# Linear attention on one core: weights cleared in eight parts, and in the tail half of a second matmul ahead of two pieces of TensorE work

## The chip, the core and the metric

The kernel runs on one core of a Trainium2 chip. A core has five engines that run side by side, each with its own instruction queue: PE (TensorE, matrix products), DVE (VectorE), ACT (ScalarE), POOL (GpSimd) and SP (SyncE, used here for issuing transfers only). Sixteen DMA engines move data between HBM and the on-chip memory (SBUF); PE writes its results to PSUM. The metric is the device time of one execution in microseconds (us), lower is better. Before the change the median of five runs is 127.72 us.

## What is computed

Linear attention over 8 x 12 = 96 heads of 512 positions and 64 features, all in fp32 at the interface:

```python
Q_feat = np.maximum(0, Q) + 1
K_feat = np.maximum(0, K) + 1
KV = np.einsum('bhkd,bhkv->bhdv', K_feat, V)
K_sum = np.sum(K_feat, axis=2)
numerator = np.einsum('bhqd,bhdv->bhqv', Q_feat, KV)
denominator = np.einsum('bhqd,bhd->bhq', Q_feat, K_sum)
return numerator / (denominator[:, :, :, None] + 1e-10)
```

Per head there is a first product (K features with V, a 64 x 64 matrix, and the sum of the K features beside it) and a second one (Q features with that matrix), and then each row is divided by its denominator.

## The kernel before

**Tiles and groups.** The 96 heads are taken in 12 groups (NG, 0 to 11) of 8 heads. Two groups make a pair, which is loaded together. Groups 2 to 9 are "eights": their Q rows are laid out so that two groups share one transposed tile, and the two groups' outputs interleave in HBM. Groups 0, 1, 10 and 11 stand by themselves.

**Steps of a group.** `k_features` and `q_features` apply max(x, 0) + 1 on DVE (written as max(x + 1, 1)). `v_blocks` spreads V into a block layout, three blocks by DVE and one by ACT. `keys_values` is the first matmul: 32 products of 64 x 320 on PE into PSUM, which ACT then casts into `kva_all`, the weights of the second matmul, four slots (`kva_diag`) used in turn. Only the diagonal blocks of a slot are written, so the rest of `kva_all` is cleared once at the start, by a memset on POOL (L274). `transposes` turns the Q features on PE, in two halves of eight transposes; ACT copies each half from PSUM to `qt`, but for the second half of group 11, which DVE copies (L213). `output` is the second matmul and the division. In each of two halves h it issues 16 matmuls of 128 x 130 into two PSUM tiles, and DVE then takes for each tile a reciprocal (L241) and a multiply (L242) into the output tile `o_sb`. There are two such PSUM tiles in all, so a half's matmuls wait for the multiplies of the half before.

**Transfers.** Loads and the stores of groups 0 to 9 are issued by POOL (L109, L119, L141); a load converts fp32 to bf16 on the way. The first K load and the stores of groups 10 and 11, each in two pieces of 512 KB, are issued by SP (L101, L144). Input tiles have two buffers per pair, output tiles six (OUT_BUFS), one for each group.

**Order.** The order on each engine is that of the program. Group g of the loop transposes what is due, makes features and V blocks of g, does the output of g - 2, the first matmul of g, issues the loads of the pair after the next, and stores g - 3. The last passes are written out:

```python
            if g == last - 1:
                v_blocks(g)
                k_features(last)
                v_blocks(last)
...
        q_features(last - 1)
        transposes(last - 1)
        q_features(last)
        output(last - 2)
        keys_values(last)
        transposes(last)
        output(last - 1)
        output(last)
```

Here `last` is 11. So PE's tail is: first matmul of 10, transposes of 10, second matmul of 9, first matmul of 11, transposes of 11, second matmul of 10, second matmul of 11.

Of the kernel before, what the change touches and what calls it, by code (L numbers as in the profile page):

```python
# [8 lines left out]
FP32 = mybir.dt.float32  # L9
BF16 = mybir.dt.bfloat16  # L10
ALU = mybir.AluOpType

BANK = 512
IN_BUFS = 2
OUT_BUFS = 6
LAG = 3


# [1 line left out]
def kernel(  # L20
# [21 lines left out]
    nc = tc.nc  # L42

    B, H, S, D = Q.shape
    P = 128
    C = 8
# [3 lines left out]
    NP = 4  # L50
    NG = NPAIR // NP
    D1 = D + 1
    W = 2 * D1
# [15 lines left out]
    mid_pool = ctx.enter_context(tc.tile_pool(name="mid", bufs=2))  # L69
    out_pool = ctx.enter_context(tc.tile_pool(name="out_pool", bufs=OUT_BUFS))  # L70
    recip_pool = ctx.enter_context(tc.tile_pool(name="recip", bufs=4))
    psum_kva = ctx.enter_context(tc.tile_pool(name="psum_kva", bufs=2, space=bass.MemoryType.PSUM))
    psum = ctx.enter_context(tc.tile_pool(name="psum", bufs=2, space=bass.MemoryType.PSUM))
# [3 lines left out]
    NV = 4  # L77
# [4 lines left out]
    kva_all = const.tile([P, NV, 4, 2, D1], BF16, name="kva_all")  # L82
    kva_diag = [kva_all[:, i] for i in range(NV)]
# [5 lines left out]
    qfs = {}  # L89
    qts = {}  # L90
    outs = {}

    def eights(g):
        return 2 <= g < NG - 2
# [4 lines left out]
    def load_first_k():  # L99
        k_raw = head_pool.tile([P, 2, C2, D], FP32, name="k_first")  # L100
        nc.sync.dma_start(out=k_raw, in_=k_dram[:, 0:2])  # L101
        raw["k", 0] = k_raw
# [29 lines left out]
                load("q", (g,))  # L132

    def store(g):
        o_sb = outs.pop(g)
        first = 2 * NP * (g // 2)
        o_to = o_dram[:, first + g % 2 : first + 2 * NP : 2] if eights(g) else o_dram[
            :, g * NP : g * NP + NP
        ]
        if g < NG - 2:  # L140
            nc.gpsimd.dma_start(out=o_to, in_=o_sb)  # L141
            return
        for h in range(2):
            nc.sync.dma_start(out=o_to[:, h:NP:2], in_=o_sb[:, h:NP:2])  # L144
# [13 lines left out]
    def v_blocks(g):  # L158
        v_raw = raw.pop(("v", g))
        for b in range(4):  # L160
            ps = slice(32 * b, 32 * b + 32)
            if b == 3:
                nc.scalar.copy(out=v_blk[g % 2][ps, b], in_=v_raw[ps])  # L163
            else:
                nc.vector.tensor_copy(out=v_blk[g % 2][ps, b], in_=v_raw[ps])  # L165
# [11 lines left out]
    def keys_values(g):  # L177
        kf = kfs.pop(g)
        sb = g % 2
        vb = v_all[:, 4 * sb : 4 * sb + 5]  # L180
        kva_ps = psum_kva.tile([P, 5, D], FP32, name="kva_ps")
        for c in range(C2):
            for n in range(2):
                nc.tensor.matmul(  # L184
                    kva_ps[64 * n : 64 * n + 64],
                    lhsT=kf[:, c, n, :],
                    rhs=vb[:, :, n, c, :],
                    start=(c == 0),
                    stop=(c == C2 - 1),
                )  # L190
        kva = kva_diag[g % NV]
        for n in range(2):
            ps = slice(64 * n, 64 * n + 64)
            nc.scalar.copy(out=kva[ps, :, n, 0:D], in_=kva_ps[ps, sb : sb + 4, :])  # L194
            nc.scalar.copy(out=kva[ps, :, n, D], in_=kva_ps[ps, 4 - 4 * sb, 0:4])  # L195

    def transposes(g):
        qf = qfs.pop(g)
        R, CC = qf.shape[1:3]
        if R == 4 and g % 2:  # L200
            qts[g] = qts[g - 1]
        else:
            qts[g] = mid_pool.tile([P, C, P, R], BF16, name=f"qt{R}")
        first = g % 2 * CC if R == 4 else 0
        for half in range(2):
            qt_ps = psum_qt.tile([P, CC // 2, R, P], BF16, name="qt_ps")
            for c in range(CC // 2):
                for r in range(R):
                    nc.tensor.transpose(  # L209
                        qt_ps[:, c, r], qf[:, r, half * CC // 2 + c, :, :], identity  # L210
                    )
            lo = first + half * CC // 2
            copy = nc.vector.tensor_copy if half and g == NG - 1 else nc.scalar.copy  # L213
            copy(out=qts[g][:, lo : lo + CC // 2], in_=qt_ps.rearrange("p c r q -> p c q r"))  # L214

    def output(g):
        qt = qts.pop(g)
        o_sb = out_pool.tile([P, NP, C, D], FP32, name="o_sb")
        for h in range(2):
            ops = [psum.tile([P, 2, BANK], FP32, tag="ps", name="o_ps") for _ in range(2)]  # L220
            for c in range(C):
                for j in range(2):
                    if eights(g):
                        b = 2 * (g % 2) + j
                        kva = kva_diag[(g // 2 * 2 + h) % NV]
                        q = slice(16 * (4 * h + b), 16 * (4 * h + b) + 16)
                    else:
                        b = 2 * h + j
                        kva = kva_diag[g % NV]
                        q = slice(32 * b, 32 * b + 32)  # L230
                    nc.tensor.matmul(  # L231
                        ops[c // 4][64 * j : 64 * j + 64, c // 2 % 2, (c % 2) * W : (c % 2) * W + W],
                        lhsT=qt[:, c, q, :],
                        rhs=kva[:, b],
                        start=True,
                        stop=True,
                    )
            for i in range(2):
                cells = ops[i][:, :, 0 : 2 * W].rearrange("p b (c n x) -> p b c n x", n=2, x=D1)
                recip = recip_pool.tile([P, 2, 2, 2, 1], FP32, name="recip")  # L240
                nc.vector.reciprocal(out=recip, in_=cells[:, :, :, :, D:D1])  # L241
                nc.vector.tensor_tensor(  # L242
                    out=o_sb[:, h:NP:2, 4 * i : 4 * i + 4].rearrange(
                        "p n (b c) d -> p b c n d", b=2
                    ),
                    in0=cells[:, :, :, :, 0:D],
                    in1=recip.to_broadcast([P, 2, 2, 2, D]),
                    op=ALU.mult,
                )
        outs[g] = o_sb  # L250

    def clear(first, split, end):
        t = v_all.rearrange("p b m c d -> p (b m c d)").bitcast(FP32)
        w = t.shape[1] // 9
        nc.vector.memset(t[:, first * w : split * w], 0.0)  # L255
        nc.scalar.copy(  # L256
            out=t[:, split * w : end * w], in_=zero.to_broadcast([P, (end - split) * w])
        )

    with tc.manual_schedule():  # L260
        nc.gpsimd.memset(zero, 0.0)
        load_first_k()
        load("v", (0,))
        load("q", (0,))
        for x in "kvq":
            load(x, (1,))
        nc.vector.memset(ones, 0.0)
        for b in range(4):
            nc.vector.memset(ones[32 * b : 32 * b + 32, b : b + 1], 1.0)  # L269
        clear(0, 3, 5)  # L270
        e = v_all[:, 4, :, :, 0:4].rearrange("p n c j -> p (n c) j")
        nc.vector.tensor_copy(out=e, in_=ones[:, None, :].to_broadcast([P, 2 * C2, 4]))
        make_identity(nc, identity)
        nc.gpsimd.memset(kva_all, 0.0)  # L274
        load_pair(1)
        clear(5, 7, 9)
        last = NG - 1
        for g in range(last):
            if g and not eights(g - 1):
                transposes(g - 1)  # L280
            elif eights(g) and g % 2:
                transposes(g - 1)
            k_features(g)
            if g < last - 1:
                v_blocks(g)
                if not eights(g):
                    q_features(g)
            if g >= 2:
                output(g - 2)
            if g == last - 1:  # L290
                v_blocks(g)
                k_features(last)
                v_blocks(last)
            if eights(g) and g % 2:
                transposes(g)
            if eights(g) and g % 2 == 0:
                q_features(g)
                q_features(g + 1)
            keys_values(g)
            if g % 2 and g // 2 + 2 < NG // 2:  # L300
                load_pair(g // 2 + 2)
            if g >= LAG:
                store(g - LAG)
        q_features(last - 1)
        transposes(last - 1)
        q_features(last)
        output(last - 2)
        keys_values(last)
        transposes(last)
        output(last - 1)  # L310
        output(last)
        for g in range(last - LAG, NG):
            store(g)
# [30 lines left out]
```

## Time and profile before

| what | value |
|---|---|
| median of five runs | 127.72 us (127.08 to 128.13) |
| profiled execution, its own time | 127.3 us |
| its span, first to last instruction | 125.5 us |
| busy PE, PE weight loads | 67.1 us (53%), 51.1 us (41%) |
| busy DVE, ACT, POOL | 90.2 us (72%), 60.4 us (48%), 27.0 us (21%) |
| PE, mean granted clock | 0.859 |
| POOL's queue | 28.84 MB, 97.5% of 16 engines' span |
| SP's queue | 3.15 MB, 6.7% |
| a store by POOL, issue to landing | 24.5 us median (9.6 to 29.8) |
| a store by SP, issue to landing | 5.2 us median (4.6 to 5.8) |
| one reciprocal, one multiply (DVE) | 200 ns, 692 ns |
| copy of half a `qt` on ACT, on DVE | 1015 ns, 1224 ns |
| memset of `kva_all` | 1825 ns |

The profile shows one execution. Busy time counts an engine's instructions, without those that only issue transfers. The page also cuts the span into 40 slices of 3.1 us and gives for each the busy share of each engine in tenths, the granted clock of PE, the busy share of the DMA engines and the rate at which they wrote. A transfer's bytes are counted as written: a load that converts to bf16 counts half of what it reads. The chain of waits follows the work that ended last back from step to step.

### The profile page before, as it was taken

To read this page: it belongs to the slowest core of one execution; us is meant where nothing else is said; L and a number is where in the kernel's file an instruction comes from. 1 tells how busy PE (TensorE), PEld (TensorE's weight loads), DVE (VectorE), ACT (ScalarE), POOL (GpSimd) and SP (SyncE) were. 2 spreads that over 40 slices of the span, in tenths; PEclk is the share of its full clock that TensorE was granted. 3 is DMA by queue.
4 is the path that set the end of the run, shared out by engine and by line. 5 is a ranking of instruction groups with operands and counts; after the bars stand their busy time and mean duration, and the time that the engine had idled before them with its cause. 6 is when DMAs were issued, how large, how long until landed. Compare 5 with 4: busy or idle time off the path is not lost.

```text
span 125.5 us, 2332 instructions
## 1 busy us (share of the span) xinstructions
PE 67.1 (53%) x960; PEld 51.1 (41%) x960; DVE 90.2 (72%) x189; ACT 60.4 (48%) x86; POOL 27.0 (21%) x39
## 2 busy tenths in 40 slices
PE   0004925940793928639776580079595088773400
PEld 0003614730572827437574470056383056552200
DVE  4897280207999899998899930899958896849910
ACT  7841094176029880866538770601992465360000
POOL 6990204000020630226202240214020300020000
PEclk9999995595589999995999999756999959999755
DMA  3999999999999999999999999999999999999991
GB/s 94 330 212 210 212 206 210 210 217 212 209 210 213 221 211 208 212 211 221 249 413 292 202 213 217 218 363 372 217 212 215 210 284 418 423 413 416 404 393 67
DMA packets 12363, 32.12 MB, mean 256 GB/s; under 512 B 577, under 2 KB 577, under 8 KB 12353
## 3 DMA queue, kind: packets, MB, share of 16 engines
q0 software_dynamic: 10992, 28.84, 97.5%
q1 hardware_dynamic: 1360, 3.15, 6.7%
q8 instruction: 7, 0.11, 0.3%
q14 instruction: 4, 0.02, 0.0%
HBM read 37.75 MB, written 12.58 MB: 401 GB/s over the span
## 4 chain that ended last, share of the span: by engine, by line
DMA 50%; DVE 19%; PE 13%; ACT 6%; issue 5%; POOL 1%; POOLq 0%; DVEq 0%
DMA v_raw<-in_V_dram 50%; PE kva_ps L184 9%; DVE o_sb L242 9%; DVE v_all L165 7%; PE qt_ps L209 3%; ACT v_all L163 3%; DVE recip L241 2%; ACT qt L214 2%; DVE qf L147 1%; PE o_ps L231 1%; ACT kva_all L194 1%; POOL v_raw L109 1%; POOL q_raw L109 1%; DVE kf L147 1%; ACT kva_all L195 0%
## 5 line engine op out<-in xcount | busy, mean ns | idle before, releaser
L184 PE MATMUL kva_ps<-v_all,kf 128*64 128x320 bf16 x384 | 37.2, 361 | 19.2 <-DVE v_all L165 14.9
L184 PEld LDWEIGHTS <-kf 128*64 128x64 bf16 x384 | 26.5, 134 | 27.0 <-DVE v_all L165 16.6
L231 PE MATMUL o_ps<-kva_all,qt 128*64 128x130 bf16 x384 | 19.0, 233 | 32.3 <-DVE o_sb L242 20.3
L165 DVE COPY v_all<-v_raw 32x2048 bf16<-32x2048 bf16 x36 | 26.3, 730 | 12.8 <-DMA v_raw<-in_V_dram 12.4
L242 DVE TENSOR_TENSOR o_sb<-o_ps,recip 128x512 f32<-128x512 f32 x48 | 33.2, 692 | 1.6
L231 PEld LDWEIGHTS <-qt 128*64 128x64 bf16 x384 | 13.1, 114 | 37.5 <-DVE o_sb L242 24.0
L163 ACT COPY v_all<-v_raw 32x2048 bf16<-32x2048 bf16 x12 | 22.6, 1894 | 10.5 <-DMA v_raw<-in_V_dram 10.4
L194 ACT CAST kva_all<-kva_ps 64x256 bf16<-64x256 f32 x24 | 8.9, 371 | 38.0 <-PE kva_ps L184 37.9
L214 ACT COPY qt<-qt_ps 128x1024 bf16<-128x1024 bf16 x23 | 22.2, 1015 | 2.8 <-PE qt_ps L209 2.5
L141 POOL DMA_DIRECT2D out_dram<-o_sb x10 | 8.8, 884 | 31.7 <-DVE o_sb L242 20.1
L147 DVE TENSOR_SCALAR kf<-k_raw 128x1024 bf16<-128x1024 bf16 x22 | 8.7, 439 | 8.5 <-DMA k_raw<-in_K_dram 8.5
L209 PE MATMUL qt_ps<-identity,qf 128*128 128x128 bf16 x192 | 13.9, 230 | 0.0
L209 PEld LDWEIGHTS <-qf 128*128 128x128 bf16 x192 | 11.8, 103 | 2.7 <-issue 1.6
L109 POOL DMA_DIRECT2D k_raw<-in_K_dram x6 | 4.7, 780 | 33.0 <-DVE kf L147 33.0
L241 DVE RECIPROCAL recip<-o_ps 128x8 f32<-128x8 f32 x48 | 9.6, 200 | 1.9 <-PE o_ps L231 1.7
L147 DVE TENSOR_SCALAR qf<-q_raw 128x1024 bf16<-128x1024 bf16 x24 | 9.0, 432 | 0.3 <-DMA q_raw<-in_Q_dram 0.3
L109 POOL DMA_DIRECT2D v_raw<-in_V_dram x7 | 5.4, 766 | 17.0 <-ACT v_all L163 16.5
L255 DVE MEMSET v_all<- 128x3072 f32 (+1 forms) x2 | 4.4, 2192 | 1.1 <-DVE ones L269 0.7
L195 ACT CAST kva_all<-kva_ps 64x4 bf16<-64x4 f32 x24 | 4.1, 169 | 0.0
L256 ACT COPY v_all<-zero 128x2048 f32<-128x2048 f32 x2 | 3.7, 1894 | 0.0
L109 POOL DMA_DIRECT2D q_raw<-in_Q_dram x4 | 2.9, 723 | 1.3 <-DMA k_raw<-in_K_dram 1.3
L119 POOL DMA_DIRECT2D q_raw<-in_Q_dram x4 | 2.8, 705 | 0.0
(14 smaller groups left out, 7.8 us busy)
## 6 DMA issues: line engine op xcount, KB each, us to landing
out_dram<-o_sb POOLq DMA_DIRECT2D x10, 1024.0 KB, 24.5
k_raw<-in_K_dram POOLq DMA_DIRECT2D x5, 1024.0 KB, 21.9
v_raw<-in_V_dram POOLq DMA_DIRECT2D x5, 1024.0 KB, 23.2
q_raw<-in_Q_dram POOLq DMA_DIRECT2D x4, 1024.0 KB, 26.0
q_raw<-in_Q_dram POOLq DMA_DIRECT2D x4, 512.0 KB, 21.4
out_dram<-o_sb SPq DMA_DIRECT2D x4, 512.0 KB, 5.2
k_first<-in_K_dram SPq DMA_DIRECT2D x1, 1024.0 KB, 4.7
v_raw<-in_V_dram POOLq DMA_DIRECT2D x2, 512.0 KB, 9.2
```

What stands on the lines that cost most here:

```text
L109: nc.gpsimd.dma_start(out=bufs[x, s][:, ms], in_=drams[x][:, 2 * groups[0] : 2 * groups[-1] + 2])
L141: nc.gpsimd.dma_start(out=o_to, in_=o_sb)
L147: nc.vector.tensor_scalar(out=dst, in0=src, scalar1=1.0, scalar2=1.0, op0=ALU.add, op1=ALU.max)
L163: nc.scalar.copy(out=v_blk[g % 2][ps, b], in_=v_raw[ps])
L165: nc.vector.tensor_copy(out=v_blk[g % 2][ps, b], in_=v_raw[ps])
L184: nc.tensor.matmul(kva_ps[64 * n : 64 * n + 64], lhsT=kf[:, c, n, :], rhs=vb[:, :, n, c, :], start=(c == 0), stop=(c == C2 - 1),)
L194: nc.scalar.copy(out=kva[ps, :, n, 0:D], in_=kva_ps[ps, sb : sb + 4, :])
L209: nc.tensor.transpose(qt_ps[:, c, r], qf[:, r, half * CC // 2 + c, :, :], identity)
L214: copy(out=qts[g][:, lo : lo + CC // 2], in_=qt_ps.rearrange("p c r q -> p c q r"))
L231: nc.tensor.matmul(ops[c // 4][64 * j : 64 * j + 64, c // 2 % 2, (c % 2) * W : (c % 2) * W + W], lhsT=qt[:, c, q, :], rhs=kva[:, b], start ...
L241: nc.vector.reciprocal(out=recip, in_=cells[:, :, :, :, D:D1])
L242: nc.vector.tensor_tensor(out=o_sb[:, h:NP:2, 4 * i : 4 * i + 4].rearrange("p n (b c) d -> p b c n d", b=2), in0=cells[:, :, :, :, 0:D], i ...
```

## The change

Four things change.

1. The weights `kva_all` are cleared by eight memsets on POOL, one for each slot and half, where one memset cleared all.
2. `output` is split into `out_matmuls` (the 16 matmuls of a half) and `norms` (its reciprocals and multiplies). In the tail, the first half of group 9's matmuls is issued on PE after the output of group 8, ahead of the first matmul of group 10; and the first half of group 10's matmuls is issued ahead of the transposes of group 11. All other matmuls keep their order.
3. ACT copies the second half of group 11's transposes too.
4. Output tiles are allocated per pair of groups, three buffers of twice the size. For the eights the two groups interleave in the pair's tile, so that a group's data is four pieces of 2 KB per partition at a step of 4 KB, where it was 8 KB in one piece. Each group keeps its own store.

```diff
-OUT_BUFS = 6
+OUT_BUFS = 3
...
-            copy = nc.vector.tensor_copy if half and g == NG - 1 else nc.scalar.copy
-            copy(out=qts[g][:, lo : lo + CC // 2], in_=qt_ps.rearrange("p c r q -> p c q r"))
+            nc.scalar.copy(out=qts[g][:, lo : lo + CC // 2], in_=qt_ps.rearrange("p c r q -> p c q r"))
+
+    def out_matmuls(g, h):
+        if h == 0:
+            open_outputs(g)
+        qt = qts[g]
+        ops = [psum.tile([P, 2, BANK], FP32, tag="ps", name="o_ps") for _ in range(2)]
+        cells_of[g, h] = ops
...
+    def open_outputs(g):
+        if g % 2 == 0:
+            outs[g // 2, "pair"] = out_pool.tile([P, 2 * NP, C, D], FP32, name="o_sb")
+        pair = outs[g // 2, "pair"]
+        o_sb = pair[:, g % 2 : 2 * NP : 2] if eights(g) else pair[:, g % 2 * NP : g % 2 * NP + NP]
+        outs[g] = o_sb
+
+    def norms(g, h):
+        ops = cells_of.pop((g, h))
+        o_sb = outs[g]
...
     def output(g):
...
+            out_matmuls(g, h)
+            norms(g, h)
...
-        nc.gpsimd.memset(kva_all, 0.0)
+        for t in kva_diag:
+            for n in range(2):
+                nc.gpsimd.memset(t[:, :, n], 0.0)
...
             if g == last - 1:
+                out_matmuls(g - 1, 0)
                 v_blocks(g)
...
         q_features(last)
-        output(last - 2)
+        norms(last - 2, 0)
+        out_matmuls(last - 2, 1)
+        norms(last - 2, 1)
         keys_values(last)
+        out_matmuls(last - 1, 0)
+        norms(last - 1, 0)
         transposes(last)
-        output(last - 1)
+        out_matmuls(last - 1, 1)
+        norms(last - 1, 1)
         output(last)
```

The bodies of `out_matmuls` and `norms` are the loops that stood in `output`, unchanged.

## The prediction

> **What bounds the kernel now.** I read the 40 slices of the page first, then the traffic lines, then windows of one microsecond over the tail, and the chain of waits last.
>
> ```profile
> DVE  4897280207999899998899930899958896849910
> DMA  3999999999999999999999999999999999999991
> GB/s 94 330 212 210 212 206 210 210 217 212 209 210 213 221 211 208 212 211 221 249 413 292 202 213 217 218 363 372 217 212 215 210 284 418 423 413 416 404 393 67
> HBM read 37.75 MB, written 12.58 MB: 401 GB/s over the span
> ```
>
> No compute engine is full throughout, but the 16 DMA engines stand at 9 in every slice between the first and the last. The GB/s line looks as if their rate halved and doubled. It counts bytes written: a load reads fp32 and writes bf16, so 212 written is 424 read; stores run at 413 to 423. The floor of the transfers is therefore 37.75 MB / 424 GB/s + 12.58 MB / 413 GB/s = 89.0 + 30.5 = 119.5 us. They start at about 2.5 us and are full to 122, which is 119.5 us: there is no hole in between that better compute could fill. Now the end, by windows (columns: stretch, its length, busy time and instruction count of PE, PEld, DVE, ACT, POOL, then granted clock, DMA share, GB/s):
>
> ```profile
> 109.00:110.00 1.00, 1.00 (x20) 0.83 (x16) 0.57 (x1) 0.00 (x0) 0.14 (x1) 1.00 1.07 438
> 110.00:111.00 1.00, 1.00 (x18) 0.72 (x15) 0.00 (x0) 0.42 (x2) 0.62 (x1) 1.00 1.01 414
> ...
> 119.00:120.00 1.00, 0.00 (x0) 0.00 (x0) 0.59 (x1) 0.00 (x0) 0.00 (x0) 0.50 1.05 406
> 120.00:121.00 1.00, 0.00 (x0) 0.00 (x0) 0.00 (x0) 0.00 (x0) 0.00 (x0) 0.50 1.05 408
> 121.00:122.00 1.00, 0.00 (x0) 0.00 (x0) 0.00 (x0) 0.00 (x0) 0.00 (x0) 0.50 1.04 406
> 122.00:123.00 1.00, 0.00 (x0) 0.00 (x0) 0.00 (x0) 0.00 (x0) 0.00 (x0) 0.50 0.64 248
> ```
>
> DVE finishes at 119.6 and SP issues the last 512 KB store there. The DMA engines stay full for 2.4 us more. That store alone takes 0.524 MB / 413 GB/s = 1.27 us, so some 1.2 us of older work was still queued when it came; with the part-filled window after 122 it is nearer 1.7. A transfer on SP's queue moves its first packet 1.1 us after issue (k_first: issued 0.74, first packet 1.81 in the packet records). The cover is thin, 0.1 to 0.6 us, but it holds. DVE's holes (the 0.57 and 0.00 above) cost nothing today.
>
> **The change, part by part.** Sums are against the profiled execution: span 125.5 us inside 127.3 us, 0.4 below the median of the five runs, 127.72.
>
> *Eight clears.* One POOL memset of 2080 elements goes, eight of 260 come. Nearest rows:
>
> ```profile
> 5.56 1.82 POOL L274 MEMSET kva_all<- 128x2080 bf16 x1
> 7.33 0.91 POOL L109 DMA_DIRECT2D k_raw<-in_K_dram  x1
> ```
>
> At the long memset's rate plus 0.1 us (the 128x1 memset's time) one part is 260 x 0.88 ns + 0.1 = 0.33 us, eight are 2.6. At the rate of the 128x128 memset (0.26 us, 2.0 ns an element) one is 0.53 and eight 4.2. If they overlap, as the 0.10 us constants that start 0.04 us apart do, the sum stays near 1.8. So the three loads behind them on POOL's queue (pair 1's k, v, q) are issued 0 to 2.4 us later; I take 0.8, the nearer row. The cover: pair 1's k, issued at 7.3, can start only when the loads ahead of it are through, and the last of them (group 1's q) lands at 17.7: about 9 us. A part would have to take over 1.3 us each to show. ACT's first cast into the weights now waits for one part only, but it starts at 15.4, long after. Cost 0.
>
> *Output buffers: three pairs instead of six singles.* The footprint is the same. The first multiply into a reused pair waits for both stores of the pair three before, where it waited for one. Landings here are those of the trace's completion records, last engine. Group 6: stores of 0 and 1 have landed by 68.9 and it multiplies at 81.4. Group 8: stores of 2 and 3 by 89.0, it multiplies at 95.1. Group 10: store of 5 lands at 108.8; its multiply moves from 113.0 to about 110.2, as worked out below, so 1.4 us remain. Behind it on DVE stands the rest of the tail; if the cover went, DVE would idle by the missing part and still end earlier than now. Cost 0. The eight middle stores now read 2 KB pieces at a 4 KB step from SBUF instead of 8 KB in one; that is the rival below.
>
> *The copy of group 11's second half* moves from DVE (1.22 us) to ACT (1.0 us, the mean of its 23). ACT is idle in the tail but for the casts. Both copies then end near 112.8; group 11's second half of columns is multiplied only after 113.4, when its PSUM is free. Cost 0 on ACT, 1.2 us less on DVE.
>
> *Half of group 9's matmuls ahead of group 10's first matmul.* 16 matmuls (0.65 us) go where PE has
>
> ```profile
> 101.01 3.72 PE L184 MATMUL kva_ps<-v_all,kf 128*64 128x320 bf16 x32 [3.89 <-DVE v_all L165]
> ```
>
> in front of it: 3.9 us of idling. Their PSUM is freed by group 8's multiplies (97.6 and 98.4) and their qt by ACT at 94.1, so they end near 98.8, 2.2 us before group 10's first matmul can start. Free. On DVE the normalization of group 9 then needs nothing from PE: it starts at 105.2, behind the q features, instead of 106.12: 0.94 us.
>
> *Half of group 10's ahead of group 11's transposes.* With everything 0.94 earlier, keys_values(11) ends at 109.6 (110.54 now). PSUM is free from 108.7, so group 10's 16 matmuls run 109.6 to 110.2, and DVE takes the first 0.44 us after they begin (as 105.66 to 106.12 shows): 110.0 instead of 112.78. Transposes shift to 110.2 to 111.3; the second half of group 10 is ready at 111.7, just as DVE is through with the first. From there eight multiplies and reciprocals at 0.84 us each run without a hole: 6.8 us, the same as the 112.78 to 119.59 of now. DVE ends at 116.8 instead of 119.6: **2.8 us earlier**, and the stores of groups 9, 10 and 11 are issued 0.9 to 2.8 us earlier.
>
> *What is late next?* The transfers. At 110 us stores of groups 6 to 9 are in flight or queued and those of 10 and 11 still to come: to the end of the trace 413 GB/s x 12.6 us = 5.2 MB. Issuing them earlier lengthens the queue and moves no byte sooner. The last byte stays at about 123.9. Sum: **0 us**.
>
> **A rule against the trace, twice.** (1) The row: queue 1 got its first store packet at 116.8 in the packet records, 2.3 us after its issue at 114.6, once group 9's store had left the faster engines. The Trainium skill (DMA: Bandwidth & Descriptors, "Queues, rings and completion order") has each engine take turns between queues packet by packet. By the rule SP's stores, now issued near 112, share with group 8's and 9's stores and those land later; by the row they wait behind. Both sums are 0, since the same bytes fill the same engines. (2) The same page ("Why small descriptors are slow") charges about 3 cycles a packet: 2048 B are 64 beats, 4096 B are 128. Today POOL's stores go as 4096 B packets, SP's as 2048 B ones, and the strided pairs could make POOL's small as well. By the rule 134 beats against 131: 2.3% of eight stores of 2.5 us, +0.46 us. By the row, a megabyte takes 2.51 us from POOL (landing to landing) and 2.53 from SP: +0.02 each, +0.2 us.
>
> **Rivals.**
> - *The chain is right and DVE sets the end* (4%). The chain of waits closes with DVE's multiplies up to 119.6. Then the whole 2.8 us come off: 124.9 on the median. Against it: a DMA share of 1.0 in each window to 122.
> - *The thin cover fails in some executions* (16%). In the profiled run PE had full clock from 104 to 117, but half clock in other stretches; at half, keys_values(11) (2.3 us) and two sets of transposes (1.1 each) add some 4 us to the tail, DVE ends later than the queue lasts, and the run is one of the 128.1. The new order has 2.8 us more cover. Then the slow runs come down to the quick ones: 127.0, 0.6% less. Against it: only the spread of the five runs hints at it.
> - *Slower* (10%): the strided pairs break POOL's stores into 2048 B packets. Place: eight stores of groups 2 to 9, on a full DMA. By packet times (84 ns against 160 for twice the bytes, 16 big packets per engine and store) 32 x 84 - 16 x 160 = 128 ns a store, +1.0 us: 128.7. By the landings +0.2. It decides from +0.08 us a store on. Against it: both descriptions move 2 KB pieces on the HBM side as before.
> - *The clears starve the start* (1%): parts over 1.3 us each; 0.5 us gives 128.2.
>
> **The numbers.** The forecast (69%) is no change by the sum: 127.3 + 0 in the profiled execution, and the median 0.4 above it, 127.7; I take 127.6, as a little of the second rival is likely in any case. Its own range is 127.1 to 128.1, the spread of the runs shown. The range to hold 8 in 10 takes in the thin cover and the cheaper end of the strided stores: 126.9 to 128.3. A measurement here tells 0.5% (0.64 us) from nothing. Faster: 16% + 4%, less the part of the second rival that stays under 0.5%, plus the edge of the first case: 0.19. Slower: 0.11. Same: 0.70.
>
> **What would show it.** DMA at 9 in every slice but the first and the last; DVE's last multiply near 116.8 and its hole before group 10 gone; SP's last store issued near 117 and landing some 7 us later, not 4.6; POOL's pair 1 loads about 0.8 us later with k landing at the same 22.7. The forecast is wrong if the last store lands much before 124, if POOL's stores show more packets than 256 a megabyte together with a longer tail, or if a slice inside falls below 9.

## The result, and the profile after

| | kernel before | kernel after |
|---|---|---|
| median | 127.22 us (72 runs, 126.76 to 128.56) | 126.8 us (43 runs, 126.36 to 128.03) |
| ratio to before | | 0.9963 (95%: 0.9951 to 0.9975) |
| span of the profiled execution | 125.5 us | 124.6 us |
| DVE's last multiply ends | 119.6 us | 116.4 us |
| SP's last store issued | 119.6 us | 116.5 us |
| last byte landed | 124.2 us | 123.7 us |
| from there to the end of the span | 1.28 us | 0.90 us |

A store has landed with its last completion record in the trace, here and below; landings and starts given to a hundredth of a microsecond are from the trace's records. The kernel after is faster by 0.37% in these runs, about 0.45 us. That is under the 0.5% that the prediction counted as no change, but its interval leaves 1 out. 126.8 us lies just below the forecast range, 126.9 to 128.3, and 0.8 us below the forecast itself, 127.6. Some 0.5 us of that is the base: the forecast was put on the first five runs of the kernel before, median 127.72, and 72 runs have 127.22.

The page of the kernel after, slices and traffic:

```profile
DVE  4898280206999899998899940799967999779300
...
DMA  3999999999999999999999999999999999999993
...
q0 software_dynamic: 10992, 28.84, 97.9%
...
HBM read 37.75 MB, written 12.58 MB: 404 GB/s over the span
```

The DMA engines are full from the second slice to the last but one, as before. POOL's queue moved the same 28.84 MB in the same 10992 packets, so the strided pairs did not break its stores into smaller ones. The timeline of the kernel after (start, duration, engine, line, operation; in brackets the idle time before it):

```profile
5.56 2.11 POOL L292 MEMSET kva_all<- 128x260 bf16 x8
...
7.62 0.90 POOL L110 DMA_DIRECT2D k_raw<-in_K_dram  x1
...
100.87 4.01 PE L185 MATMUL kva_ps<-v_all,kf 128*64 128x320 bf16 x32 [1.98 <-DVE v_all L166]
...
109.20 0.62 PE L232 MATMUL o_ps<-kva_all,qt 128*64 128x130 bf16 x16
...
109.64 0.21 DVE L253 RECIPROCAL recip<-o_ps 128x8 f32<-128x8 f32 x1 [1.24 <-PE o_ps L232]
...
115.75 0.69 DVE L254 TENSOR_TENSOR o_sb<-o_ps,recip 128x512 f32<-128x512 f32 x1
```

The eight clears take 2.11 us for 1.82, and pair 1's first load starts 0.29 us later. PE waits 1.98 us instead of 3.89 ahead of group 10's first matmul, since half of group 9 now runs in that gap. In the kernel before, DVE's first and last step of groups 10 and 11 were

```profile
112.78 0.20 DVE L241 RECIPROCAL recip<-o_ps 128x8 f32<-128x8 f32 x1
...
118.90 0.69 DVE L242 TENSOR_TENSOR o_sb<-o_ps,recip 128x512 f32<-128x512 f32 x1
```

so DVE now begins group 10 at 109.64 instead of 112.78 and is done 3.1 us earlier. SP's stores (durations, first and last issue, then the time from issue to landing) in the kernel before:

```profile
L144 SPq DMA_DIRECT2D out_dram<-o_sb x4: 372/373/382, 114.6 to 119.6; - x4
...
DMA to landing us min/median/max: 4.6/5.2/5.8
```

and in the kernel after, with its last microseconds by windows (columns as in the prediction):

```profile
L145 SPq DMA_DIRECT2D out_dram<-o_sb x4: 372/372/382, 111.4 to 116.5; - x4
...
DMA to landing us min/median/max: 7.3/7.9/8.4
```

```profile
116.00:117.00 1.00, 0.00 (x0) 0.00 (x0) 0.45 (x1) 0.00 (x0) 0.00 (x0) 0.50 1.05 424
117.00:118.00 1.00, 0.00 (x0) 0.00 (x0) 0.00 (x0) 0.00 (x0) 0.00 (x0) 0.50 1.00 401
...
121.00:122.00 1.00, 0.00 (x0) 0.00 (x0) 0.00 (x0) 0.00 (x0) 0.00 (x0) 0.50 0.98 381
122.00:123.00 1.00, 0.00 (x0) 0.00 (x0) 0.00 (x0) 0.00 (x0) 0.00 (x0) 0.50 0.59 229
123.00:124.00 1.00, 0.00 (x0) 0.00 (x0) 0.00 (x0) 0.00 (x0) 0.00 (x0) 0.50 0.06 21
```

The stores were issued 3.1 us earlier and waited 2.7 us longer. The transfers end at nearly the same time: the work saved on DVE is hidden behind a full queue. So where do 0.4 us come from? The two profiles differ in two terms behind DVE's end: the last landing (0.49 us) and the stretch from it to the end (0.38 us). The second has a visible place: the closing code, in which the engines wait for each other once more behind the last landing. The profile shows each step of such a wait as an EVENT_SEMAPHORE or a DRAIN, and marks records that do not count as busy by a q (POOLq, PEldq). Lines of it (count, duration in ns, first and last start), in the kernel before:

```profile
L339 POOLq EVENT_SEMAPHORE  x4: 17/17/17, 124.4 to 125.4; - x4
...
L339 POOLq DRAIN  x2: 51/72/92, 124.5 to 124.8; - x2
L339 POOLq EVENT_SEMAPHORE_RANGE_CLEAR  x1: 135/135/135, 124.7 to 124.7; - x1
L339 PEldq DRAIN  x1: 13/13/13, 124.7 to 124.7; - x1
```

and in the kernel after:

```profile
L363 POOLq EVENT_SEMAPHORE  x4: 17/17/17, 123.9 to 124.5; - x4
...
L363 POOLq DRAIN  x2: 51/72/93, 124.1 to 124.3; - x2
L363 POOLq EVENT_SEMAPHORE_RANGE_CLEAR  x1: 135/135/135, 124.2 to 124.2; - x1
```

POOL runs the same closing instructions in both. In the kernel before, its second drain starts at 124.8 and takes 51 ns, yet the last two events come only at 125.3 and 125.4: from 124.886 to 125.299 there is a hole of 0.41 us. In the kernel after the same step takes 0.04 us. POOL did not wait for another engine there: the others were through with their part by 124.7, PE as the last (its drain in the lines above). The other engines' last waits end with POOL's last event, so the hole is on the path.

### The profile page after: what moved, and what is told of

The parts are those of the page before. It is cut to its first block, busy times and chain, and to the rows that moved or that the text cites. A ratio compares the mean times of both kernels' runs of the same rounds, so it can differ in the third digit from the quotient of the medians.

```text
span 124.6 us, 2342 instructions
## 1 busy us (share of the span) xinstructions
PE 69.5 (56%) x960; PEld 52.9 (42%) x960; DVE 89.0 (71%) x188; ACT 61.3 (49%) x87; POOL 27.4 (22%) x46
## 3 DMA queue, kind: packets, MB, share of 16 engines
q0 software_dynamic: 10992, 28.84, 97.9%
## 4 chain that ended last, share of the span: by engine, by line
DMA 50%; DVE 23%; PE 8%; ACT 6%; issue 5%; POOL 2%; POOLq 0%; DVEq 0%
DMA v_raw<-in_V_dram 50%; DVE o_sb L254 9%; DVE v_all L166 9%; PE kva_ps L185 7%; ACT v_all L164 3%; DVE qf L148 2%; DVE recip L253 2%; ACT qt L214 2%; DVE kf L148 1%; PE qt_ps L210 1%; ACT kva_all L195 1%; PE o_ps L232 1%; POOL v_raw L110 1%; POOL q_raw L110 1%; ACT kva_all L196 0%
## 5 line engine op out<-in xcount | busy, mean ns | idle before, releaser
L185 PE MATMUL kva_ps<-v_all,kf 128*64 128x320 bf16 x384 | 38.8, 372 | 17.8 <-DVE v_all L166 13.3
L185 PEld LDWEIGHTS <-kf 128*64 128x64 bf16 x384 | 27.6, 138 | 26.1 <-DVE v_all L166 14.7
L232 PE MATMUL o_ps<-kva_all,qt 128*64 128x130 bf16 x384 | 19.5, 235 | 28.2 <-DVE o_sb L254 17.3
L214 ACT COPY qt<-qt_ps 128x1024 bf16<-128x1024 bf16 x24 | 23.1, 1015 | 3.1 <-PE qt_ps L210 2.8
```

The lines of the kernel that those rows point to most:

```text
L185: nc.tensor.matmul(kva_ps[64 * n : 64 * n + 64], lhsT=kf[:, c, n, :], rhs=vb[:, :, n, c, :], start=(c == 0), stop=(c == C2 - 1),)
L214: nc.scalar.copy(out=qts[g][:, lo : lo + CC // 2], in_=qt_ps.rearrange("p c r q -> p c q r"))
L232: nc.tensor.matmul(ops[c // 4][64 * j : 64 * j + 64, c // 2 % 2, (c % 2) * W : (c % 2) * W + W], lhsT=qt[:, c, q, :], rhs=kva[:, b], start ...
```

## The experiments

Two theories stood against each other. **Closing theory:** the hole at POOL's end depends on how many instructions POOL's program has (the profile counts 70 POOL records before and 77 after, the seven extra clears), and the new order brings nothing. **Tail theory:** earlier stores end the transfers earlier, or cover executions in which they came too late. A third, smaller one, **pair theory:** the paired buffers change the rate of the stores. Each ratio below is to runs of the kernel before taken in the same session.

### The kernel before again, and the parts alone

> The kernel before once more, as a second profile and as a measure of the noise. Between the two first profiles two terms differ: the last landing (124.21 before, 123.72 after) and the stretch from the last landing to the end of the span (1.28 before, 0.90 after, with a hole of 0.41 us between two of POOL's closing instructions that the kernel after does not have). Closing theory: 1.28 comes back within 0.05 us, and the last landing scatters by some 0.3 us. Tail theory (stores issued earlier end the transfers earlier): the last landing is 124.2 again within 0.1. Ratio 1.000 within 0.002 by either.

Measured: ratio 1.0019 (0.9996 to 1.0042). Landing to end 1.29. The last landing came at 124.29, but in another way than in the first profile:

```profile
L144 SPq DMA_DIRECT2D out_dram<-o_sb x4: 372/372/382, 116.4 to 121.6; - x4
...
DMA to landing us min/median/max: 2.7/3.1/3.8
```

```profile
118.00:119.00 1.00, 0.68 (x9) 0.40 (x8) 0.96 (x4) 0.00 (x0) 0.00 (x0) 0.50 0.88 336
...
120.00:121.00 1.00, 0.55 (x8) 0.30 (x8) 0.96 (x3) 0.00 (x0) 0.00 (x0) 0.50 0.65 252
121.00:122.00 1.00, 0.00 (x0) 0.00 (x0) 0.53 (x1) 0.00 (x0) 0.00 (x0) 0.50 1.06 414
122.00:123.00 1.00, 0.00 (x0) 0.00 (x0) 0.00 (x0) 0.00 (x0) 0.00 (x0) 0.50 0.64 248
```

The same program ended on DVE at 121.5, not 119.6, and SP's last store landed 2.7 us after its issue, not 4.6. The DMA share falls to 0.65: some engines waited for stores. In this execution group 9's first matmul ended at 96.5 and not at 94.6, beside a granted PE clock of 0.64 from 93 to 97 us (1.00 in the first profile), and all behind it came late. Yet the last landing hardly moved, 124.29 for 124.21.

> The kernel before with the eight clears and nothing else: seven instructions more on POOL. Closing theory (POOL's instruction count moves a stall at the very end): landing to end about 0.90 us instead of 1.28, ratio about 0.997. Tail theory and pair theory: ratio 1.000, landing to end 1.28.

```diff
-        nc.gpsimd.memset(kva_all, 0.0)
+        for t in kva_diag:
+            for n in range(2):
+                nc.gpsimd.memset(t[:, :, n], 0.0)
```

Landing to end: 0.90, no hole. Ratio 0.9993 (0.9977 to 1.0009): the profile speaks for the closing theory, the times did not tell.

> The kernel after with one clear again; the new order, the pairs and the copy on ACT stay. Closing theory: the gain goes, ratio about 1.000, landing to end 1.28. Tail theory: the gain stays, ratio about 0.996, DVE's last multiply near 115.8 and the last landing near 123.7.

```diff
-        for t in kva_diag:
-            for n in range(2):
-                nc.gpsimd.memset(t[:, :, n], 0.0)
+        nc.gpsimd.memset(kva_all, 0.0)
```

Landing to end: 1.28, the hole is back. DVE ended at 116.4, last landing 123.96. Ratio 0.9989 (0.9973 to 1.0004): smaller than the gain of the whole, but not clearly 1 either.

> The kernel before with three paired output buffers and nothing else. Pair theory (reading 2 KB pieces at a step of 4 KB changes the rate of the stores): ratio other than 1.000 and a megabyte of POOL's stores lands at another spacing than 2.51 us. Closing and tail theory: ratio 1.000, POOL's stores still 256 packets a megabyte, landing to end 1.28.

```diff
-OUT_BUFS = 6
+OUT_BUFS = 3
...
-        o_sb = out_pool.tile([P, NP, C, D], FP32, name="o_sb")
+        if g % 2 == 0:
+            outs[g // 2, "pair"] = out_pool.tile([P, 2 * NP, C, D], FP32, name="o_sb")
+        pair = outs[g // 2, "pair"]
+        o_sb = pair[:, g % 2 : 2 * NP : 2] if eights(g) else pair[:, g % 2 * NP : g % 2 * NP + NP]
```

Ratio 1.0002 (0.9985 to 1.002). Stores of groups 4 to 8 landed 2.50 to 2.51 us apart (first engine), as before. The pairs cost and bring nothing.

### Is it the count, and where is the hole?

> The kernel before, one clear, and behind it seven memsets of a single unused element on POOL: POOL's instruction count is that of the kernel after, nothing else is. Closing theory (the count, not the shape of the clears): landing to end 0.90 us as in both kernels with eight clears, against 1.27 to 1.29 in the four with one; ratio about 0.997. If it is the clears themselves: 1.28 and 1.000.

```diff
         nc.gpsimd.memset(kva_all, 0.0)
+        for _ in range(7):
+            nc.gpsimd.memset(pad, 0.0)
```

`pad` is an unused tile of one element per partition. Landing to end: 0.90. In the profile, seven instructions without any use do what the eight clears did. Ratio 0.9986 (0.9971 to 1.0001): the times do not tell 0.997 from 1 here.

> The kernel before with two unused memsets on POOL. If POOL stalls at a fixed place of its program (as at the edge of a block of instructions), two more ahead push the hole two closing instructions forward: it stands in front of the range clear instead of in front of the last but one semaphore event, still about 0.4 us, landing to end still about 1.28. If the count only decides yes or no: 0.90 or 1.28 with the hole at the old place.

> The kernel before with five unused memsets on POOL. By the fixed place the hole falls in front of POOL's wait for the other engines at the end, while POOL has nothing to do but wait for the last landing: hidden, landing to end 0.90 as with seven. By a threshold between six and seven: 1.28.

With two unused memsets POOL's part of the closing code reads:

```profile
L342 POOLq EVENT_SEMAPHORE  x4: 17/17/17, 124.6 to 125.6; - x4
...
L342 POOLq DRAIN  x2: 51/76/101, 124.7 to 125.4; - x2
L342 POOLq EVENT_SEMAPHORE_RANGE_CLEAR  x1: 135/135/135, 125.2 to 125.2; - x1
```

The first drain starts at 124.7 and takes 101 ns, and the range clear comes only at 125.2: the hole of 0.40 us now stands in front of the range clear, two instructions ahead of its old place, and the second drain and the last event follow without one. Landing to end is 1.28 still. With five, no hole is left:

```profile
L342 POOLq EVENT_SEMAPHORE  x4: 17/17/17, 124.6 to 125.3; - x4
...
L342 POOLq DRAIN  x2: 51/76/101, 124.8 to 125.1; - x2
...
L342 POOLq EVENT_SEMAPHORE_RANGE_CLEAR  x1: 135/135/135, 124.9 to 124.9; - x1
```

Landing to end is 0.91. By the same count, the place now stands five instructions earlier, ahead of POOL's wait for the other engines, where POOL idles for microseconds in any case. So the stall belongs to a fixed place in POOL's program, and what counts is whether POOL passes it while the other engines wait for POOL. (The runs with two and five were profiled once each and not timed further.) It holds in every profile of the study: the eight with 70 or 72 POOL records have 1.27 to 1.29 us from landing to end, the nine with 77 and the one with 75 have 0.90 or 0.91.

### How much cover do the stores have?

To see the tail at work, DVE was held up ahead of group 10's V blocks in both orders:

```diff
             if g == last - 1:
+                for _ in range(2):
+                    nc.vector.memset(pad, 0.0)
                 v_blocks(g)
```

> The kernel before with two memsets of an unused tile on DVE (2.62 us each) ahead of group 10's V blocks; some 0.4 us of them fall into DVE's wait there. Everything behind on DVE and PE comes about 4.8 us later. Tail theory with a cover (the end is the later of the transfers' own end, 124.2, and SP's last issue plus about 2.6 us): last issue 124.4 to 126.3, last landing 127.0 to 128.9, time 129.9 to 131.8. Transfers alone: unchanged, 127.2.

> The kernel after with the same two memsets at the same place. Its DVE ended at 116.5, so now at 121.3, SP's last issue with it; plus 2.6 us is 123.9, still inside the transfers' own end. Tail theory with a cover: time 126.8 to 127.2, 3 us or more below the kernel before with the same delay. Without a cover both kernels are late alike by 4.8 us: 131.6.

> As the one before, but group 11's transposes stand ahead of group 10's first half again; group 9's half stays ahead, and the copy stays on ACT. The sixteen transposes (1.1 us) come back between keys_values and group 10's matmuls: DVE ends 1.1 us later than in the run above, near 122.4, last landing near 125.0, time 0.7 to 1.1 us above the run above.

The hold was longer than reckoned, since each memset also stood 0.6 to 0.7 us behind an idle gap: some 6.5 us and not 4.8 in the kernel after. So the times of the kernels before and after lie above what was expected (132.34 us for 129.9 to 131.8, 128.46 for 126.8 to 127.2), and the kernel after used up its cover too. The third run lies 0.96 us above the second, as expected. SP's stores in the kernel before with the hold:

```profile
L145 SPq DMA_DIRECT2D out_dram<-o_sb x4: 372/372/382, 121.7 to 126.8; - x4
...
DMA to landing us min/median/max: 2.7/2.7/2.8
```

and two of its windows:

```profile
121.00:122.00 1.00, 0.58 (x16) 0.42 (x15) 0.97 (x3) 0.00 (x0) 0.00 (x0) 0.96 0.02 8
122.00:123.00 1.00, 0.58 (x14) 0.37 (x9) 0.97 (x3) 0.00 (x0) 0.00 (x0) 0.50 0.39 152
```

and the stores of the kernel after with the hold:

```profile
L146 SPq DMA_DIRECT2D out_dram<-o_sb x4: 372/372/382, 118.0 to 123.0; - x4
...
DMA to landing us min/median/max: 2.7/3.2/3.8
```

A share of 0.02 is an empty queue: here DVE does set the end.

| kernel | last store issued | last landing | between | median us |
|---|---|---|---|---|
| before, first profile | 119.61 | 124.21 | 4.60 | 127.22 |
| before, again | 121.55 | 124.29 | 2.74 | 127.4 |
| after | 116.47 | 123.72 | 7.25 | 126.8 |
| before, held | 126.83 | 129.57 | 2.74 | 132.34 |
| after, held | 122.99 | 125.74 | 2.75 | 128.46 |
| after, held, group 10's half undone | 124.24 | 126.98 | 2.74 | 129.42 |

(The medians with the hold are of four, six and four runs.) The last landing is the later of two things: the transfers' own end, 123.7 to 124.7 us, and the last issue plus 2.74, which is what a store takes when nothing is queued ahead of it. They meet when the last issue comes at about 121.3. Once the queue is empty, the new order is worth what it saves on DVE: 3.8 us in the landings of these two profiles. The times differ by 3.9, but that holds the closing stretch too, 1.28 against 0.91. Undoing group 10's half costs 1.24 in the landing and 0.96 in the time. Without the hold the new order issues its last store at 116.4 to 117.8, far ahead of 121.3. The old order does so at 119.6 to 121.6: in three of its nine profiles the last landing came 2.74 to 2.80 us after the last issue, so the cover was just used up, but the landing, 124.0 to 124.4, was no later than in the others.

### The two parts in one table

> The kernel after once more, beside the next run. If its gain is the closing stretch (0.37 us) and a little from the cover: ratio 0.9963 again within 0.002, landing to end 0.90, SP's last issue near 116.5, last landing 123.7 to 124.5.

> The kernel after with one clear and seven memsets of one unused element behind it: new order, pairs, ACT copy, POOL's count of the kernel after, but not its clears. Closing theory: the same as the kernel after, ratio about 0.996, landing to end 0.90, and about 0.37 us below the kernel after with one clear alone (127.1). If the eight clears themselves bring something: near 127.1.

Measured: ratio 0.9989 (0.9969 to 1.0008) for the kernel after again, less of a gain than expected, and 0.9989 (0.9969 to 1.0009) with seven unused memsets in place of its clears. Landing to end 0.91 and 0.90. Neither the gain nor its absence shows in these times. The medians are 126.89 and 127.1 us. 127.1 is what was expected if the clears themselves brought something, but the two ratios are equal, and the table below has the unused memsets at 0.9970 beside the clears at 0.9973. So order and count were crossed and timed side by side:

> First of four in one table: old order, POOL's old count. The zero of the table: ratio 1.000, landing to end 1.28.

> Old order, seven unused memsets on POOL. If the closing stretch is the larger part: 0.37 us less, ratio 0.997. If the order is: ratio 0.999 or more. Landing to end 0.90.

> New order, one clear. If the thin cover costs the old order 0.1 to 0.3 us on the median and more in its slowest runs: ratio 0.998 to 0.999, and the slowest tenth of its runs below 127.6 where the old order's is near 127.8. Landing to end 1.28.

> New order, eight clears. If both parts add: ratio 0.995 to 0.997, the lowest of the four. Landing to end 0.90.

| | POOL's old count | seven more |
|---|---|---|
| old order | 0.9999 (0.9983 to 1.0015), 127.13 us | **0.9970** (0.9955 to 0.9986), 126.9 us |
| new order | 1.0008 (0.999 to 1.0027), 127.27 us | **0.9973** (0.9956 to 0.999), 126.9 us |
| landing to end | 1.28, 1.28 | 0.91, 0.90 |

In each column the two orders agree; in each row the two counts differ. By the means of the 22 runs in each cell, seven more instructions take off 0.22 us in the old order and 0.41 in the new, 0.31 on the average (95%: 0.20 to 0.43), which has room for the 0.37 us of the closing stretch. The new order takes nothing that can be seen: +0.06 us (-0.06 to 0.17). Taken together with the other timed runs without a hold the picture is the same: with the seven more, the ratios of all seven comparisons lie at 0.9963 to 0.9993, on the mean 0.9980, and with the old count, of all five, at 0.9989 to 1.0019, on the mean 1.0003. So the 0.37% of the first comparison is the upper end of what the kernel after showed (0.9989 and 0.9973 when it was timed again).

The new order's last landing, 124.1 on the mean of six profiles (123.72 to 124.74), stands beside 124.3 for nine of the old order (123.86 to 124.52), which is no clear difference. Sorted by the count instead, the same profiles give 124.1 and 124.3 as well, so neither can be credited with it, and the 0.49 us between the first two profiles' landings are within the scatter. The guess that the slowest tenth of runs would show the cover (below 127.6 in the new order) fell too: with one clear it was 127.78 in the new order and 127.46 in the old.

## Why the prediction was right in most steps and missed the gain

- **What bounds the kernel.** Right. In every profile without the hold the DMA engines stand at 9 up to the last slices (three profiles of the old order, those whose cover was used up, show 8 there), and DVE's saving vanished behind them. This part of the forecast was right by its mechanism and not by luck.
- **Half of groups 9 and 10 ahead.** Right in place and size: DVE's end was forecast at 116.8 and came at 116.4; SP's last issue near 117, at 116.5, landing 7.3 us later where 7 was said. One line was careless: the hole before group 10 did not go, it shrank to 1.24 us, as the working's own times (group 9 through at 108.7, group 10 from 110.0) say.
- **Pairs and the copy on ACT.** Right: no cost, the same packets. The copy was not run alone; in the kernel after, DVE works without a hole from 109.64 to its end behind it.
- **"Eight clears. Cost 0."** This is the step that failed. The cost at the start was sized well (the eight take 2.11 us where 2.6 were said, and pair 1's k still lands at 23.1, hidden). But the sum ended there. Seven more instructions also move the rest of POOL's program against a fixed place at which POOL stalls 0.41 us, and in the kernel before that place lay among the last instructions, behind the last landing, where nothing hides it. The term was -0.38 us in the profiles, -0.31 in the times of the table, and the sum put it at nothing without a look.
- **What follows the last byte as a constant.** This is the same failure from its other side. The prediction left the last byte at about 123.9 and made the sum 0 from that. It never looked at the 1.28 us between the last landing (124.21) and the end, 1% of the kernel, although the hole of 0.41 us stands in the trace of the kernel before.
- **The base.** 127.72 was the median of five runs, and half a microsecond too high. So of the 0.8 us between 127.6 and 126.8 the larger part, 0.5, is the base; the missing term and scatter are the rest. That the error of the base and the missing term pointed the same way was bad luck.
- **Rivals.** DVE does not set the end. The cover: counted by the last landing (time from the last issue to it, less the 2.74 us of an empty queue) it was 1.9 us in the profiled execution, more than the 0.1 to 0.6 said, but 0 to 1.4 us in the eight other profiles of the old order without a hold, where the last issue came at 120.3 to 121.6. So the rival saw rightly that other executions have less. Its price was not there. The 16 DMA engines do not finish a store together: of the last store, the first engine was done at 122.31 and the last at 124.21 in the first profile of the kernel before, but at 124.07 and 124.29 in the second, where the last issue came late. So the engines that are ahead lose their lead first, and the last landing hardly moves. Smaller packets and a starved start did not occur; even with pair 1's first load issued at 10.03, behind seven unused memsets, it landed as before.
- **The two rules.** On turns between queues: in the kernel after, SP's first store packet came 3.5 us after issue, and over the next microseconds POOL's and SP's packets went out about one for one (34 of 4096 B and 37 of 2048 B in half a microsecond, in the packet records). So both the wait and the turns are there; the sum was 0 by either. On small packets: POOL's packets stayed as they were, so neither the estimate of +0.46 us by the rule nor the +0.2 us by the row was put to the test.

## What to carry to other kernels

Where transfers fill the span, as here, work saved on an engine in the tail is hidden as long as the last store is issued while enough older work is queued. Measure that cover by holding the engine up, not from one profile: here one profile showed 1.9 us of it and another none. Split the end of a profile into last landing and closing, and compare the closing before and after: seven instructions more on POOL moved it by 0.37 us here. A difference of 0.3 to 0.4% between two kernels can lie in instructions that do nothing, so cross the parts of a change in one table before crediting one.

## What had not been expected of the hardware

POOL stalls for 0.40 to 0.41 us at a fixed place of its program; two instructions put ahead of it move the stall by exactly two. In each profile with the visible stall a fetch of 8 KB appears 0.7 to 1.0 us after the stall's end, behind the end of the kernel, on queue q14, whose kind the page gives as instruction. In those with seven more instructions such a fetch stands at 102 to 104 us instead, where POOL waits for group 9's last multiply, and at 122 with five. So the fetch moves with the place. But it starts when the stall is over, so the stall is not the wait for its bytes.

That fits the edge of a block of instructions. The Trainium skill (Runtime: NRT & Kernel Launch, "Instruction fetch mechanics") has instructions stream in by blocks of 16 KiB and calls the cost of a block's edge mostly hidden. If the stall is such an edge, it was hidden here only where POOL had something to wait for, and 0.37 us of the time where it had not. The fetch seen here is of 8 KB. That the stall is such an edge is argued from these places and was not shown by a run of its own, and what POOL does in the 0.4 us stays open.
